# Triangular inverses of the first mixer in three blocks of 42 and 43 rows, with two applications of W, and a new order of the work around them

## The chip, the cores and the metric

The kernel runs on one core of a Trainium2 chip. Its engines work side by side, each on its own queue of instructions: TensorE (PE; its weight loads are shown apart, as PEld), VectorE (DVE), ScalarE (ACT), GpSimd (POOL) and SyncE (SP), which issues most DMAs. The metric is the device time of one execution in microseconds. Every run of the kernel before took between 2796.86 and 2800.05 us.

## The reference

Two layers on 256 tokens of width 2048, in float32. The first layer's mixer is a gated DeltaNet; the change is in that mixer alone. Cut to what matters:

```python
proj = x @ w_in                                  # q, k, v, z, and two gates per value head
qkv = silu(causal_dwconv(qkv, conv_w))           # 16 q/k heads, 32 value heads, 128 wide
q = l2norm(q) * 128 ** -0.5; k = l2norm(k)
gc = cumsum(g)                                   # log-decay within a chunk
lmat = where(strict, (beta * k) @ k.T * exp(gc_i - gc_j), 0)
sol = solve_triangular(I + lmat, [beta * v, beta * k * exp(gc)], lower, unit_diagonal)
# then a scan over chunks with state S, an RMS norm of o, times silu(z), times w_o
```

The two layers go on with LayerNorm, a convolutional GLU, a gated embedding, a second mixer with sparse attention, and again a GLU and the embedding.

## The kernel before

**Weights and matmuls.** A weight chunk of 512 KB is loaded by SP into one of four `raw` tiles, split by ACT into a rounded part `hi` and by DVE into the remainder `lo` (L114, L115; three buffers each), and used by PE. `gemm_t_steps` (L147 with `hi`, L151 with `lo`; tile `mm_ps`) makes transposed products, `gemm_steps` (L184, L187, L190; tile `b_ps`) plain ones. A scheduler sets the order on every engine when the program is built, by its own costs; on the chip each queue runs strictly in that order.

**The mixer.** 32 value heads are worked in eight groups of four (`g` = 0 to 7). The 256 tokens are two halves (`a` = 0, 1) of 128, so that each group has eight triangular matrices `L` of 128x128 (two halves, four heads). For a group: `keys` (gemms for k and q), `zgate` (the z gemm), `values` (the v gemm), and between them the attention arithmetic:

- `decays` and `sums` make decay factors and the norms from the Gram matrix of k (`gram`, L542 and L543); `blocks` finishes `L` on DVE (L574) and sends the four diagonal blocks of 32x32 of each matrix to DRAM (`lt`, four DMAs) and back (`ld`, four DMAs) so that 128 partitions hold 32 blocks in four copies. All eight DMAs stand in SP's queue, among the weight loads.
- `substitute` inverts the blocks on POOL: 31 columns, for each a product `xt` (L612) and a subtraction (L614), starting from an identity `xi` that POOL copies from constants (L609). Four DMAs write the result to `tt`.
- `inverses` brings it back as block-diagonal matrices `pm` (four DMAs on POOL's queue, L631), multiplies `L` by them on PE (`w_ps`, L623) and keeps what lies above the diagonal blocks as `W` (ACT, L638).
- `solve` then needs, for each half, y0 = `pm` x rhs, and three times y = y0 - W y (a product on PE, L623, tile `s_ps`, and a subtraction on DVE, L691): with four blocks in a row, W to the fourth power is zero. The second half waits for the first (`n21`).
- `causal` and `mixes` make the masked q-k products; `outputs` makes o and its norm; its transposes run later as `rest`.

In the loop the work of group n = s+1 that leads to its substitution (`front(n)`) is written after `inverses(s)`, that is, behind the z gemm of group n. A float32 matmul of the attention part (128x128, not rounded) shows as two records in the trace.

Of the kernel before, what the change touches and what calls it, by code (L numbers as in the profile page):

```python
# [30 lines left out]
C_IDENT, C_TRI, C_QMIN, C_CMIN, C_CAUSAL, C_XINIT, C_ONES = 0, 128, 256, 384, 512, 640, 896  # L31
N_CONST = 1024


def constants():

    c = np.zeros((P, N_CONST), np.float32)
    i, j = np.arange(P)[:, None], np.arange(P)[None, :]
    c[:, C_IDENT:C_IDENT + P] = i == j
    c[:, C_TRI:C_TRI + P] = i <= j  # L40
    c[:, C_CMIN:C_CMIN + P] = np.where(j <= i, np.float32(3.4e38), np.float32(-BIG))
    x = np.zeros((4, 32, 8, 32), np.float32)
    for cg in range(4):
        for k in range(8):
            x[cg, :, k, 4 * k + cg] = 1.0
    c[:, C_XINIT:C_XINIT + 256] = x.reshape(P, 256)
    c[:, C_ONES:C_ONES + P] = 1.0
# [16 lines left out]
class Trunk:  # L64
    def __init__(self, nc, tc, ctx, t):

        self.low_last = False
        self.nc, self.tc, self.t = nc, tc, t
        pool = lambda **k: ctx.enter_context(tc.tile_pool(**k))

        self.const = pool(name="const", bufs=1)
        self.hl = pool(name="hl", bufs=3)
        self.xtp = pool(name="xtp", bufs=1)
        self.big = pool(name="big", bufs=1)
        self.cp = pool(name="cp", bufs=1, side="right")
# [289 lines left out]
    def gdn_gates(self, pool, w, gk):  # L365
# [42 lines left out]
        nc.tensor.matmul(pc[:, 64:96], self.ones, g[:, 0], start=True, stop=True)  # L408
# [8 lines left out]
    def gdn(self, ahead):  # L417
# [3 lines left out]
        with tc.tile_pool(name="gk", bufs=1) as gk, tc.tile_pool(name="gw", bufs=1) as pool:  # L421
# [5 lines left out]
            cr = pool.tile([64, 4, P], F32, tag="ld", name="cr")  # L427
            w = pool.tile([P, 1024], F32, tag="L", name="gates")
            def load(nb, to=None):

                for a in range(2):
                    nc.sync.dma_start(out=xs[nb][:, a], in_=t["x"][a * P:(a + 1) * P, nb * 512:(nb + 1) * 512])
                for a in range(2):
                    self.halves = self.to_xT(self.xT, xs[nb][:, a], a, nb * 4, to)
                later = {0: [(w[:, 256 + 32 * i:288 + 32 * i], bass.AP(tensor=t[k].tensor, offset=t[k].offset,
                                                                       ap=[[0, P], [1, 32]]))
                             for i, k in enumerate(("gdn_dt_bias", "gdn_a_log"))],
                         1: [(cr, t["gdn_conv_w"].rearrange("k (n c) -> n k c", c=P)), (self.cst, t["cst"][:, P:]),
                             (ng, t["gdn_norm_g"].rearrange("(p o) -> p o", o=1))]}.get(nb, ())
                for out, src in later:  # L440
                    self.after(nc.gpsimd.dma_start(out=out, in_=src), self.turned, sync=True)
# [11 lines left out]
    def gdn_groups(self, pool, gk, cw, ng, oT, load, taps, gates, ahead):  # L453
# [7 lines left out]
        nc.gpsimd.memset(pm, 0.0)  # L461
        W = pool.tile([P, 2, 4, P], F32, tag="W", name="W")
# [22 lines left out]
        def decays(s):  # L485
# [5 lines left out]
            L = s["L"] = pool.tile([P, 2, 4, P], F32, tag="L", name="L")  # L491
# [4 lines left out]

        def causal(s):

            g, dm = s["g"], s["qd"]
            do = s["qo"] = pool.tile([P, 4, P], F32, tag="qo", name="qo", bufs=2)  # L500
            for h in h4:
                nc.scalar.activation(do[:, h], dm[:, 1, h], AF.Exp, bias=self.gout[:, 4 * g + h:4 * g + h + 1])
            n21 = s["n21"] = pool.tile([P, 4, P], F32, tag="n21", name="n21", bufs=2)
            nc.vector.tensor_tensor(five(n21), bcast(s["gram"][0][:, :, P:S], 2, 2), five(do), op=ALU.mult)
# [5 lines left out]
            sq = s["sq"] = pool.tile([P, 2, S], F32, tag="y0", name="sq")  # L510
            nc.scalar.activation(sq, s["q"], AF.Square)
# [34 lines left out]
        def sums(s):  # L546
# [3 lines left out]
            ss, ik = small("ss", 4), small("ik", 4)  # L550
# [17 lines left out]
        def blocks(s):  # L568
# [8 lines left out]
            lt = self.dr.tile([8, 4, 32, 32], F32, tag="lt", name="lt")  # L577
            for b in range(4):
                nc.sync.dma_start(out=lt[:, b].rearrange("q i j -> i q j"),
                                    in_=L[32 * b:32 * b + 32, :, :, 32 * b:32 * b + 32].rearrange("p a h j -> p (a h) j"))  # L580
            ld = s["ld"] = pool.tile([P, 32, 32], F32, tag="ld", name="ld")
            for e in h4:
                nc.sync.dma_start(out=ld[32 * e:32 * e + 32], in_=bass.AP(tensor=lt.tensor, offset=lt.offset,
                                                                          ap=[[1024, 32], [1, 1024]]))

        def mixes(s):
# [6 lines left out]

            pss = self.sp.tile([P, 4], F32, tag="sp", name="ss_ps")
            for h in range(2):
                for a in range(2):
                    nc.tensor.matmul(pss[:, 2 * h + a:][:, 0:1], s["sq"][:, h, a * P:(a + 1) * P],
                                     self.ones[:, 0:1], start=True, stop=True)
# [4 lines left out]
        def substitute(s):  # L603


            ld = s["ld"]
            xi = pool.tile([P, 8, 32], F32, tag="xi", name="xi", bufs=2)
            tmp = pool.tile([P, 8, 32], F32, tag="xt", name="xt", bufs=2)
            nc.gpsimd.tensor_copy(xi, self.xinit.rearrange("p (c j) -> p c j", c=8))  # L609
            for i in range(31):  # L610
                w, m = 31 - i, i // 4 + 1
                nc.gpsimd.tensor_tensor(tmp[:, :m, :w], bcast(ld[:, i + 1:, i], m, 1),  # L612
                                        xi[:, :m, i:i + 1].to_broadcast([P, m, w]), op=ALU.mult)
                nc.gpsimd.tensor_tensor(xi[:, :m, i + 1:], xi[:, :m, i + 1:], tmp[:, :m, :w], op=ALU.subtract)  # L614
            tt = s["tt"] = self.dr.tile([8, 4, 8, 4, 32], F32, tag="tt", name="tt")
            for e in range(4):
                nc.gpsimd.dma_start(out=tt[:, :, :, e].rearrange("q b c j -> (q b) c j"), in_=xi[32 * e:32 * e + 32])
# [10 lines left out]
        def inverses(s):  # L628

            for b in range(4):  # L630
                nc.gpsimd.dma_start(out=pm[32 * b:32 * b + 32, :, 32 * b:32 * b + 32],  # L631
                                    in_=s["tt"][:, b].rearrange("q c e j -> (c e) q j"))
            for a in range(2):
                ps = self.sp.tile([P, 4, 96], F32, tag="bk", name="w_ps")
                mul(s["L"][:, a], pm[:, 4 * a:4 * a + 4, 32:], ps)

                for b in (1, 2, 3):
                    nc.scalar.activation(W[:32 * b, a, :, 32 * b:32 * b + 32], ps[:32 * b, :, 32 * b - 32:32 * b], AF.Copy)  # L638

        def values(s):  # L640
            g = s["g"]
            v = pool.tile([P, 4, S], F32, tag="v", name="v")
            steps = self.gemm_t_steps(w_in, 4096 + 512 * g, 512, self.xT, conv(32 + 4 * g, lambda n: v[:, n]))
            if not g:
# [18 lines left out]
        def zgate(s, rest):  # L663
# [7 lines left out]
            for j, _ in enumerate(self.gemm_steps(w_in, 8192 + 512 * s["g"], 512, lambda k: self.xT[:, k], KT, done)):  # L671
                if j > 2 and rest:
                    rest.pop(0)()

        def solve(s):
            vt = s["vt"]
            u = s["u"] = pool.tile([P, 2, 4, P], F32, tag="u", name="u")
            for a in range(2):
# [55 lines left out]
        def front(s):  # L734
# [455 lines left out]
```

## Time and profile before

| | us |
|---|---|
| median of three runs (2796.86, 2797.15, 2800.05) | 2797.15 |
| the profiled execution's own time | 2797.12 |
| its span from first to last instruction | 2795.1 |
| PE busy / PEld busy | 2776.6 / 2390.1 |
| DVE busy / ACT busy / POOL busy | 1856.2 / 1421.6 / 337.7 |
| POOL busy in 143 to 228 us (one group's length) | 32.57 |

A busy PE is not PE at its peak: the ends of matmuls are modelled, and neighbours overlap. What one matmul costs is read from the distance of the starts in the timeline. The trace has the device's granted TensorE clock at 1.00 all along.

### The profile page before, as it was taken

To read this page: it belongs to the slowest core of one execution; us is meant where nothing else is said; L and a number is where in the kernel's file an instruction comes from. 1 tells how busy PE (TensorE), PEld (TensorE's weight loads), DVE (VectorE), ACT (ScalarE), POOL (GpSimd) and SP (SyncE) were. 2 spreads that over 40 slices of the span, in tenths; PEclk is the share of its full clock that TensorE was granted. 3 is DMA by queue.
4 is the path that set the end of the run, shared out by engine and by line. 5 is a ranking of instruction groups with operands and counts; after the bars stand their busy time and mean duration, and the time that the engine had idled before them with its cause. 6 is when DMAs were issued, how large, how long until landed. Compare 5 with 4: busy or idle time off the path is not lost. (4 is left out here: it accounts for less than half of the span.)

```text
span 2795.1 us, 40216 instructions
## 1 busy us (share of the span) xinstructions
PE 2776.6 (99%) x14958; PEld 2390.1 (86%) x14958; DVE 1856.2 (66%) x3059; ACT 1421.6 (51%) x2239; POOL 337.7 (12%) x688
## 2 busy tenths in 40 slices
PE   8999999999999999999999999999999999999999
PEld 7888888888888888888888889888888888888887
DVE  6787787877556666666545665776676666655566
ACT  4555566555445555555434544455465555543453
POOL 1543234442200000000000000120000000000000
PEclk9999999999999999999999999999999999999999
DMA  7755665655565666666556567655556666665655
GB/s 213 205 157 158 166 176 164 168 152 159 173 210 164 193 206 206 207 196 207 196 191 208 171 198 215 181 152 163 181 181 196 197 187 199 194 195 195 207 171 195
DMA packets 412275, 520.82 MB, mean 186 GB/s; under 512 B 28940, under 2 KB 301712, under 8 KB 411824
## 3 DMA queue, kind: packets, MB, share of 16 engines
q1 hardware_dynamic: 404912, 499.91, 58.9%
q0 software_dynamic: 7168, 18.35, 2.7%
q8 instruction: 117, 1.92, 0.3%
q14 instruction: 78, 0.64, 0.1%
HBM read 513.94 MB, written 7.39 MB: 187 GB/s over the span
## 5 line engine op out<-in xcount | busy, mean ns | idle before, releaser
L115 DVE TENSOR_TENSOR lo<-raw,hi 128x1024 fp32r<-128x1024 f32 (+1 forms) x921 | 1125.0, 1223 | 606.0 <-ACT hi L114 594.6
L114 ACT ACTIVATE hi<-raw 128x1024 fp32r<-128x1024 f32 (+1 forms) x921 | 967.9, 1053 | 698.9 <-PE b_ps L187 469.5
L147 PE MATMUL mm_ps<-xT,hi 128*128 128x512 f32 (+1 forms) x4176 | 1027.9, 394 | 2.6 <-ACT hi L114 2.3
L147 PEld LDWEIGHTS mm_ps<-xT,hi 128*128 128x128 f32 (+1 forms) x4176 | 762.0, 188 | 148.9 <-ACT hi L114 2.9
L151 PEld LDWEIGHTS mm_ps<-xT,lo 128*128 128x128 f32 (+1 forms) x4176 | 539.4, 191 | 22.7 <-DVE lo L115 1.5
L151 PE MATMUL mm_ps<-xT,lo 128*128 128x256 f32 (+1 forms) x4176 | 557.2, 284 | 0.4 <-DVE lo L115 0.4
L184 PE MATMUL b_ps<-hi,xT 128*128 128x512 f32 (+1 forms) x704 | 270.9, 386 | 0.0
L187 PE MATMUL b_ps<-hi,xT 128*128 128x512 f32 (+1 forms) x704 | 268.8, 383 | 0.0
L220 ACT ACTIVATE fold<-mm_ps 128x256 f32<-128x256 f32 x261 | 98.1, 376 | 268.1 <-PE mm_ps L147 267.8
L184 PE MATMUL b_ps<-hi,hTA 128*128 128x512 f32 x512 | 199.3, 389 | 0.0
L187 PE MATMUL b_ps<-hi,hTA 128*128 128x512 f32 x512 | 199.2, 389 | 0.0
L190 PE MATMUL b_ps<-lo,xT 128*128 128x512 f32 (+1 forms) x704 | 188.4, 383 | 0.0
L239 POOL DMA_DIRECT2D lng<-in_ln_g x16 | 8.8, 547 | 1239.1 <-PE b_ps L190 654.5
L612 POOL TENSOR_TENSOR xt<-ld,xi 128x60 f32<-128x60 f32 (+24 forms) x248 | 116.2, 468 | 345.1 <-DMA ld<-lt 326.3
L187 PEld LDWEIGHTS b_ps<-hi,xT 128*128 128x128 f32 x704 | 132.2, 188 | 24.8
L184 PEld LDWEIGHTS b_ps<-hi,xT 128*128 128x128 f32 x704 | 132.2, 188 | 24.1
L190 PEld LDWEIGHTS b_ps<-lo,xT 128*128 128x128 f32 x704 | 129.9, 188 | 24.5
L190 PE MATMUL b_ps<-lo,hTA 128*128 128x512 f32 x512 | 136.8, 389 | 0.0
L190 PEld LDWEIGHTS b_ps<-lo,hTA 128*128 128x128 f32 x512 | 96.1, 188 | 20.0
L184 PEld LDWEIGHTS b_ps<-hi,hTA 128*128 128x128 f32 x512 | 96.1, 188 | 20.0
L187 PEld LDWEIGHTS b_ps<-hi,hTA 128*128 128x128 f32 x512 | 96.1, 188 | 19.9
L614 POOL TENSOR_TENSOR xi<-xi,xt 128x60 f32<-128x60 f32 (+24 forms) x248 | 107.5, 433 | 19.4
(266 smaller groups left out, 2571.0 us busy)
## 6 DMA issues: line engine op xcount, KB each, us to landing
raw<-in_gdn_w_in SPq DMA_DIRECT2D x193, 512.0 KB, 4.4
raw<-in_ffn_w_gate SPq DMA_DIRECT2D x160, 512.0 KB, 4.4
raw<-in_ffn_w_up SPq DMA_DIRECT2D x160, 512.0 KB, 4.6
raw<-in_ffn_w_down SPq DMA_DIRECT2D x160, 512.0 KB, 4.1
raw<-in_dsa_w_in SPq DMA_DIRECT2D x72, 512.0 KB, 3.7
raw<-in_gdn_w_o SPq DMA_DIRECT2D x64, 512.0 KB, 4.0
raw<-in_ple_w_gate SPq DMA_DIRECT2D x64, 512.0 KB, 4.9
raw<-in_dsa_w_o SPq DMA_DIRECT2D x32, 512.0 KB, 3.9
```

Source lines behind the costliest of these rows:

```text
L114: act = nc.scalar.activation(hi, raw, AF.Copy)
L115: ins = nc.vector.tensor_tensor(lo, raw, hi.bitcast(F32), op=ALU.subtract)
L147: ins = nc.tensor.matmul(q[:m, :], hi[:, k, o:o + m], x[:, k0 + k].rearrange("p a b -> p (a b)"), start=k0 + k == 0, stop=last)
L151: ins = nc.tensor.matmul(q[:m, S:], lo[:, k, o:o + m], x[:, k0 + k, 0, :], start=False, stop=last)
L184: ins = nc.tensor.matmul(ps[a][:, :n], xh, hi, start=k == 0, stop=False)
L187: self.before = nc.tensor.matmul(ps[a][:, :n], xl, hi, start=False, stop=False)
L190: self.last = nc.tensor.matmul(ps[a][:, :n], x(k)[:, 0, a * P:(a + 1) * P], lo, start=False, stop=k == kt - 1)
L220: nc.scalar.activation(t[:m], ps[:, S:], AF.Copy)
L239: ins = self.nc.gpsimd.dma_start(out=r, in_=bass.AP(tensor=src.tensor, offset=src.offset, ap=[[0, P], [1, n]]))
L612: nc.gpsimd.tensor_tensor(tmp[:, :m, :w], bcast(ld[:, i + 1:, i], m, 1), xi[:, :m, i:i + 1].to_broadcast([P, m, w]), op=ALU.mult)
L614: nc.gpsimd.tensor_tensor(xi[:, :m, i + 1:], xi[:, :m, i + 1:], tmp[:, :m, :w], op=ALU.subtract)
```

## The change

Blocks of 32 rows become blocks of 42, 43 and 43 rows (`B_FROM` = 0, 42, 85, 128). Three blocks in a row need two applications of W. The pieces:

- `substitute` runs 42 columns, 84 operations of POOL in place of 62, on up to 132 elements for each partition (76 before). Four copies of 24 blocks lie in groups of 32 partitions, of which eight carry zeros. A block's columns lie in two tiles, 22 and 21 wide, so that `lt` takes six DMAs (48 or 32 rows, pieces of 88 and 84 bytes: 1920 pieces in place of 1024 of 128 bytes), and `ld` eight in place of four.
- `xi` starts from a DMA of constants in place of a copy by POOL. `pm` comes back in three DMAs of 48 rows in place of four of 32; ACT makes two pieces of W in place of three.
- `solve` loses one of three applications in each half.
- `front(n)` now stands at the start of z's gemm of group n (`zgate(n, [], ...)`), and `L` has two buffers. For the first group's successor it stands behind that gemm, and seven of the eight steps of its v gemm are taken before `inverses(0)`.
- `causal`, `squares` and `mixes` of a group move from `front` and from behind `front` into `values`; `cross` (with its own exponentials, four more of ACT for each group) makes `n21` ahead of them. `qo`, `ld` and `ik` have one buffer, `cr` and the ones for one product sit in other tiles.

```diff
+B_ROWS, B_COLS, B_LEFT = 43, 12, 22
+B_FROM = (0, 42, 85, P)
...
-            lt = self.dr.tile([8, 4, 32, 32], F32, tag="lt", name="lt")
-            for b in range(4):
-                nc.sync.dma_start(out=lt[:, b].rearrange("q i j -> i q j"),
-                                    in_=L[32 * b:32 * b + 32, :, :, 32 * b:32 * b + 32].rearrange("p a h j -> p (a h) j"))
...
+            for lt, ld, k, n, o, tall, lead in lds:
+                for b, r in enumerate(B_FROM[:3]):
+                    c = r + o
+                    r0 = min(c, P - tall)
+                    at = lead - c + r0
+                    nc.sync.dma_start(out=lt[8 * b:8 * b + 8, at:at + tall].rearrange("q i j -> i q j"),
+                                      in_=L[r0:r0 + tall, :, :, c:c + n].rearrange("p a h j -> p (a h) j"))
+            for lt, ld, k, n, o, tall, lead in lds:
+                for e in h4:
+                    nc.sync.dma_start(out=ld[32 * e:32 * e + 32], in_=lt[:, lead:lead + k])
...
-            nc.gpsimd.tensor_copy(xi, self.xinit.rearrange("p (c j) -> p c j", c=8))
-            for i in range(31):
-                w, m = 31 - i, i // 4 + 1
...
+            xi = pool.tile([P, B_COLS, B_ROWS], F32, tag="xi", name="xi")
+            nc.gpsimd.dma_start(out=xi, in_=t["cst"][:, C_XINIT:])
+            for i in range(B_ROWS - 1):
+                w, m = B_ROWS - 1 - i, i // 4 + 1
+                col = ld[:, i + 1:, i] if i < B_LEFT else right[:, i + 1 - B_LEFT:, i - B_LEFT]
+                tmp = pool.tile([P, 132], F32, tag="xt", name="xt")[:, :m * w].rearrange("p (c j) -> p c j", c=m)
+                nc.gpsimd.tensor_tensor(tmp, bcast(col, m, 1), xi[:, :m, i:i + 1].to_broadcast([P, m, w]), op=ALU.mult)
+                nc.gpsimd.tensor_tensor(xi[:, :m, i + 1:], xi[:, :m, i + 1:], tmp, op=ALU.subtract)
...
-                for i in range(3):
+                for i in range(2):
                     ps = mul(W[:, a], y)
...
             if g < 7:
                 n = keys(g + 1, rest)
-                zgate(n, [])
+                zgate(n, [], (lambda: front(n)) if g else None)
+                if not g:
+                    front(n)
+                    for _, _ in zip(range(7), begin(n)[0]):
+                        pass
...
             inverses(s)
             if g < 7:
-                front(n)
-                mixes(n)
                 substitute(n)
             solve(s)
```

Where the scheduler now puts the instructions, at three places.

PE, second half of `solve` in the second group, from the product with `n21` to the first product of the outputs. Before (`s_ps<-y` are the applications of W, `s_ps<-vt,pm` makes y0, `mm_ps` is the v gemm of the next group between them):

```order
L623 MATMUL s_ps<-u,n_1522 128x128 x4
L147 MATMUL mm_ps<-xT,hi 128x512 x8
L623 MATMUL s_ps<-vt,pm 128x128 x4
L147 MATMUL mm_ps<-xT,hi 128x512 x2
L151 MATMUL mm_ps<-xT,lo 128x256 x2
L623 MATMUL s_ps<-y_2597,W 128x128 x4
L151 MATMUL mm_ps<-xT,lo 128x256 x8
L623 MATMUL s_ps<-y,W 128x128 x4
L151 MATMUL mm_ps<-xT,lo 128x256 x6
L147 MATMUL mm_ps<-xT,hi 128x512
L623 MATMUL s_ps<-y,W 128x128 x4
L704 MATMUL o_ps<-u,qd 128x128 x4
```

The same stretch now:

```order
L640 MATMUL s_ps<-u,n_1582 128x128 x4
L149 MATMUL mm_ps<-xT,lo 128x256 x4
L145 MATMUL mm_ps<-xT,hi 128x512 x5
L640 MATMUL s_ps<-vt,pm 128x128 x4
L145 MATMUL mm_ps<-xT,hi 128x512 x4
L640 MATMUL s_ps<-y_2761,W 128x128 x4
L145 MATMUL mm_ps<-xT,hi 128x512 x7
L149 MATMUL mm_ps<-xT,lo 128x256 x3
L640 MATMUL s_ps<-y,W 128x128 x4
L743 MATMUL o_ps<-u,qd 128x128 x4
```

One application of four matmuls is gone; between each product and the next there is still work of the v gemm.

PE, at the end of the second z gemm (`b_ps`), where the first group's inverses are first used (`w_ps`). Before:

```order
L190 MATMUL b_ps<-lo,xT 128x512 x2
L623 MATMUL w_ps<-pm,L 128x96 x8
L542 MATMUL g_ps<-k 128x256
L543 MATMUL g_ps<-k 128x128
L542 MATMUL g_ps<-k 128x256
L543 MATMUL g_ps<-k 128x128
L623 MATMUL s_ps<-vt,pm 128x128 x4
```

Now (the Gram matrix of the second group first, then 112 matmuls of its v gemm):

```order
L555 MATMUL g_ps<-k 128x256
L556 MATMUL g_ps<-k 128x128
L555 MATMUL g_ps<-k 128x256
L556 MATMUL g_ps<-k 128x128
L145 MATMUL mm_ps<-xT,hi 128x512 x8
L149 MATMUL mm_ps<-xT,lo 128x256 x16
L145 MATMUL mm_ps<-xT,hi 128x512 x16
L149 MATMUL mm_ps<-xT,lo 128x256 x16
L145 MATMUL mm_ps<-xT,hi 128x512 x16
L149 MATMUL mm_ps<-xT,lo 128x256 x16
L145 MATMUL mm_ps<-xT,hi 128x512 x16
L149 MATMUL mm_ps<-xT,lo 128x256 x8
```

Directly behind these rows follow `w_ps<-pm,L` and `s_ps<-vt,pm`: the first use of `pm` moved behind one Gram product and 56 + 56 matmuls of the v gemm. In later groups `w_ps` stands directly behind the z gemm, as before.

POOL, at the end of a substitution (`tt` goes out, `pm` comes back, the next `xi`). Before:

```order
L612 TENSOR_TENSOR xt<-ld,xi 128x8
L614 TENSOR_TENSOR xi<-xi,xt 128x8
L617 DMA tt<-xi 256x1x32 x4
L631 DMA pm<-tt 32x8x32 x4
L609 COPY xi<-cst 128x256
L612 TENSOR_TENSOR xt<-ld,xi 128x31
```

Now:

```order
L630 TENSOR_TENSOR xt<-ld,xi 128x11
L631 TENSOR_TENSOR xi<-xi,xt 128x11
L634 DMA tt<-xi 384x1x43 x4
L650 DMA pm<-tt 48x8x42
L650 DMA pm<-tt 48x8x43 x2
L625 DMA xi<-in_cst 128x516
L630 TENSOR_TENSOR xt<-ld,xi 128x42
```

One substitution follows the other on POOL as before, with a load of `xi` between them.

More of the change, by code (lines that the diff above doesn't have):

```diff
@@ L41, in constants @@
     c[:, C_CMIN:C_CMIN + P] = np.where(j <= i, np.float32(3.4e38), np.float32(-BIG))
[L42 to L47, printed above, removed]
+    x = np.zeros((4, 32, B_COLS, B_ROWS), np.float32)
+    for n in range(B_ROWS):
+        x[n % 4, :, n // 4, n] = 1.0
+    c[:, C_XINIT:] = x.reshape(P, B_COLS * B_ROWS)
     c[:, C_CAUSAL:C_CAUSAL + P] = j <= i
@@ L407, in gdn_gates @@
         nc.tensor.matmul(pc[:, 0:64], self.tri, g64, start=True, stop=True)
-        nc.tensor.matmul(pc[:, 64:96], self.ones, g[:, 0], start=True, stop=True)
+        ones = pool.tile([P, P], F32, tag="y0", name="ones")
+        nc.gpsimd.memset(ones, 1.0)
+        nc.tensor.matmul(pc[:, 64:96], ones, g[:, 0], start=True, stop=True)
         nc.tensor.matmul(pc[:64, 128:256], g64, self.tri, start=True, stop=True)
@@ L461, in gdn_groups @@
         nc.gpsimd.memset(pm, 0.0)
+        lds, nl = [], B_ROWS - B_LEFT
+        for k, n, o, tall in ((B_ROWS, B_LEFT, 0, 48), (nl, nl, B_LEFT, 32)):
+            lead = B_FROM[2] + o + tall - P
+            lt = self.dr.tile([32, lead + tall, n], F32, tag=f"lt{n}", name="lt", bufs=1)
+            ld = pool.tile([P, k, n], F32, tag=f"ld{n}", name="ld")
+            nc.gpsimd.memset(ld, 0.0)
+            nc.gpsimd.dma_start(out=lt[24:, lead:lead + k], in_=ld[:8])
+            lds.append((lt, ld, k, n, o, tall, lead))
         W = pool.tile([P, 2, 4, P], F32, tag="W", name="W")
@@ L628, in inverses, with begin @@
         def inverses(s):
-            for b in range(4):
-                nc.gpsimd.dma_start(out=pm[32 * b:32 * b + 32, :, 32 * b:32 * b + 32],
-                                    in_=s["tt"][:, b].rearrange("q c e j -> (c e) q j"))
-            for a in range(2):
[L634 to L638, printed above, removed]
+            tt, rows = s["tt"], 4 * B_COLS
+            for b, r in enumerate(B_FROM[:3]):
+                r0, w = min(r, P - rows), B_FROM[b + 1] - r
+                nc.gpsimd.dma_start(out=pm[r0:r0 + rows, :, r:r + w],
+                                    in_=bass.AP(tensor=tt.tensor, offset=tt.offset + (8 * b * rows - r + r0) * B_ROWS,
+                                                ap=[[B_ROWS, rows], [rows * B_ROWS, 8], [1, w]]))
+            r1, r2 = B_FROM[1:3]
+            for a in range(2):
+                ps = self.sp.tile([P, 4, P - r1], F32, tag="bk", name="w_ps")
+                mul(s["L"][:, a], pm[:, 4 * a:4 * a + 4, r1:], ps)
+                for r, n in ((r1, r2 - r1), (r2, P - r2)):
+                    nc.scalar.activation(W[:r, a, :, r:r + n], ps[:r, :, r - r1:r - r1 + n], AF.Copy)
+        def begin(s):
+            g = s["g"]
+            v = pool.tile([P, 4, S], F32, tag="v", name="v")
+            if "v" in s:
+                return s["v"]
+            s["v"] = self.gemm_t_steps(w_in, 4096 + 512 * g, 512, self.xT, conv(32 + 4 * g, lambda n: v[:, n])), v
+            return s["v"]
         def values(s):
             g = s["g"]
-            v = pool.tile([P, 4, S], F32, tag="v", name="v")
-            steps = self.gemm_t_steps(w_in, 4096 + 512 * g, 512, self.xT, conv(32 + 4 * g, lambda n: v[:, n]))
+            steps, v = begin(s)
             if not g:
@@ L649, in values @@
                 front(s)
+                causal(s)
                 substitute(s)
+            else:
+                causal(s)
+                if g > 1:
+                    for _ in range(3):
+                        next(steps)
+                squares(s)
+                next(steps)
+                mixes(s)
             self.go_(steps)
@@ L661, in values, with zgate @@
             return [lambda: turn(0), lambda: turn(1)]
-        def zgate(s, rest):
+        def zgate(s, rest, behind=None):
             zs = s["zs"] = pool.tile([P, 2, 512], F32, tag="zs", name="zs", bufs=2)
@@ L671, in zgate @@
             for j, _ in enumerate(self.gemm_steps(w_in, 8192 + 512 * s["g"], 512, lambda k: self.xT[:, k], KT, done)):
-                if j > 2 and rest:
+                if behind is not None and not j:
+                    behind()
+                if j > 3 and rest:
                     rest.pop(0)()
@@ L738, in front @@
                 blocks(s)
-            causal(s)
+            cross(s)
         n, rest = keys(0), []
@@ L745, in gdn_groups @@
             if not g:
-                rest.insert(0, lambda: mixes(s))
+                rest[:0] = [lambda: squares(s), lambda: mixes(s)]
                 zgate(s, rest)
```

51 lines of the change are left out of this document (22 added, 29 removed).

## The prediction

> **What bounds the kernel now.** I read the page's head first, then who PE waited for, the window of one group, and last the timeline of PE and POOL around one `solve`.
>
> ```profile
> span 2795.1 us, 40216 instructions
> PE 2776.6 (99%) x14958; PEld 2390.1 (86%) x14958; DVE 1856.2 (66%) x3059; ACT 1421.6 (51%) x2239; POOL 337.7 (12%) x688
> ```
>
> ```profile
> PE t_ps L231 <- DMA x_in<-in_x: 5.1, 1, 5.1
> ...
> PE g_ps L542 <- DVE L L574: 0.5, 1, 0.5
> ```
>
> ```profile
> 314.00:399.00 85.00, 84.95 (x504) 74.55 (x503) 66.52 (x146) 48.33 (x102) 32.38 (x71) 1.00 0.60 164
> ```
>
> The waits are for PE: who, total us, times, longest. The window gives PE, PEld, DVE, ACT and POOL busy: a group lasts some 85 us, DVE works 67 of them, ACT 49, POOL 33, and PE has no gap. PE's own issue sets the time, so a PE record that goes is a gain, and work on another engine costs only where PE comes to wait for it.
>
> A busy PE is modelled, so the price of a record is the distance of starts:
>
> ```profile
> 317.23 3.82 PE L147 MATMUL mm_ps<-xT,hi 128*128 128x512 f32 x16
> 320.89 2.08 PE L151 MATMUL mm_ps<-xT,lo 128*128 128x256 f32 x16
> 322.80 1.09 PE L147 MATMUL mm_ps<-xT,hi 128*128 128x512 f32 x4
> ...
> 330.72 1.14 PE L623 MATMUL s_ps<-y,W 128*128 128x128 f32 x8
> 331.62 1.20 PE L151 MATMUL mm_ps<-xT,lo 128*128 128x256 f32 x8
> 332.65 0.63 PE L147 MATMUL mm_ps<-xT,hi 128*128 128x512 f32 x2
> 333.12 1.05 PE L623 MATMUL s_ps<-y,W 128*128 128x128 f32 x8
> 333.93 1.17 PE L147 MATMUL mm_ps<-xT,hi 128*128 128x512 f32 x4
> 334.95 1.16 PE L623 MATMUL s_ps<-u,n 128*128 128x128 f32 x8
> ```
>
> Sixteen `hi` matmuls take 3.66 us (0.229 each), sixteen `lo` 1.91 (0.119 each). An application of W, eight records, takes 331.62 - 330.72 = 0.90, and the eight `lo` behind it take 1.03 in place of 0.95: 0.98 in all where it had to wait a moment for DVE. The one at 333.12 takes 0.81, the four `hi` behind it 1.02 in place of 0.92: 0.91.
>
> **The change part by part.**
>
> *Applications of W.* One of three goes in two halves of eight groups: 16 x (0.91 to 0.98) = 14.6 to 15.7 us of PE; I take 15.1. In the new order every product is still followed by gemm work before its reader, 0.7 us or more (six `lo` are 0.72, four `hi` 0.92), about what stood there before, so the shorter chain makes no new gap. A block of float32 work inserted elsewhere costs only its own records: the change of kind is in the figures above, and there are as many `g`, `ss` and transposing matmuls as before. `w_ps` has as many records, narrower ones.
>
> *The first q-k product.* In group 0 it came late:
>
> ```profile
> 78.30 1.07 PE L190 MATMUL b_ps<-lo,xT 128*128 128x512 f32 x4
> 79.91 0.70 PE L542 MATMUL g_ps<-q,k 128*128 128x256 f32 x2 [0.54 <-DVE L L574]
> ```
>
> Four matmuls at 0.227 end at 79.21, so PE lost 0.7. It now stands twelve and more z matmuls later (2.7 us): -0.7, at worst 0.
>
> *The substitution on POOL.* This is the part that grows.
>
> ```profile
> 337.19 0.26 POOL L612 TENSOR_TENSOR xt<-ld,xi 128x29 f32<-128x29 f32 x1
> 337.52 0.30 POOL L614 TENSOR_TENSOR xi<-xi,xt 128x29 f32<-128x29 f32 x1
> 337.90 1.21 POOL L612 TENSOR_TENSOR xt<-ld,xi 128x28 f32<-128x28 f32 x1
> ...
> 344.22 0.33 POOL L612 TENSOR_TENSOR xt<-ld,xi 128x66 f32<-128x66 f32 x1
> ...
> 346.58 0.35 POOL L612 TENSOR_TENSOR xt<-ld,xi 128x76 f32<-128x76 f32 x1
> ```
>
> ```profile
> 337.78 1.22 DVE L115 TENSOR_TENSOR lo<-raw,hi 128x1024 fp32r<-128x1024 f32 x1
> ```
>
> From 29 to 76 elements an operation goes from 0.26 to 0.35: some 2.3 ns an element on 0.18 us, with 0.08 between operations. The one at 337.90 took 1.21: it began inside DVE's split of 337.78 and ended 0.11 after it. The Trainium skill, "SBUF — State Buffer", section "SBUF: two separate sides", has this as an exclusive lock of a port pair that GpSimd shares with DVE operations with two SBUF inputs; the row agrees for POOL. By that rule a longer substitution collides with more splits; without it, it would be 38 us long, and the wait worked out below would be nought.
>
> Before, 62 operations on 2 x 1560 elements make 11.2 + 7.2 + 5.0 = 23 us, and the second group's took this long:
>
> ```profile
> 164.98 0.26 POOL L612 TENSOR_TENSOR xt<-ld,xi 128x31 f32<-128x31 f32 x1 [29.72 <-DMA ld<-lt]
> ...
> 196.84 0.32 POOL L614 TENSOR_TENSOR xi<-xi,xt 128x8 f32<-128x8 f32 x1
> 197.46 2.32 POOL L617 DMA_DIRECT2D tt<-xi  x4 [0.29 <-POOL xi L614]
> 202.42 2.33 POOL L631 DMA_DIRECT2D pm<-tt  x4 [2.64 <-PE mm_ps L147]
> ```
>
> That is 32.2 us, of which 9 lost to collisions, 0.15 an operation. Now 84 operations on 2 x 3663 elements: 15.1 + 16.8 + 6.7 = 38.6. With the loss per operation 51, with the loss as a share of the time (28%) 54: I take 52. As 52 of the 84 are larger than any in the trace, and read columns of another stride, I keep 48 to 58.
>
> From the end of a substitution to `pm` landed: 197.16 to the last issue's start at 204.17, and the landing:
>
> ```profile
> DMA to landing us min/median/max: 3.2/4.7/6.6
> ```
>
> 11.7 in all; one `pm` issue fewer (0.6) against larger pieces: kept.
>
> *Is it in time?* POOL's deadline is `w_ps` on PE:
>
> ```profile
> 138.80 1.92 PE L623 MATMUL w_ps<-pm,L 128*128 128x96 f32 x16
> 140.55 0.62 PE L542 MATMUL g_ps<-k 128*128 128x256 f32 x2
> ```
>
> ```profile
> 224.16 1.92 PE L623 MATMUL w_ps<-pm,L 128*128 128x96 f32 x16
> ```
>
> Group 0:
>
> ```profile
> 89.23 0.78 POOL L612 TENSOR_TENSOR xt<-ld,xi 128x31 f32<-128x31 f32 x1 [25.91 <-DMA ld<-lt]
> ...
> 125.28 0.22 POOL L614 TENSOR_TENSOR xi<-xi,xt 128x8 f32<-128x8 f32 x1
> ```
>
> Its deadline goes to 138.8 - 0.7 + 1.3 (Gram, four pieces) + 56 x 0.229 + 56 x 0.119 = 158.9. Its `ld` is unchanged but for two more `lt` issues, so 89.7 + 55 (this group had 36.3 us, 4 more than the next) + 11.7 = 156.4. In time by 2.5 us.
>
> Group 1: the Gram product comes at 138.1, and `ld` landed 24.4 us behind it before (140.55 to 164.98). DVE is freer there now (`causal` went), SP has more to issue; kept: 162.5. POOL is free by then: 144.7, `tt` and `pm` out at 153, `xi` in some 4 us later. 162.5 + 52 + 11.7 = 226.2. The deadline: 224.16 - 0.7 - 1.9 (two applications) + 1.3 (group 2's Gram product now stands ahead) = 222.9. PE waits 3.3 us; with 48 to 58 us nought to 9.3.
>
> Later groups: `front` runs at the start of z's gemm, some 20 us sooner before its deadline, against 20 us more of substitution. From Gram product to deadline are a period of 83.5 (85.4 from one `w_ps` above to the next, less 1.9) and 20 of the z gemm, the chain is 24.4 + 52 + 11.7 = 88: 15 us to spare. A rewritten `ld` must also wait until the last substitution has read it; SP, with weights queued behind, asks for it some 80 us after the last one, when POOL has been done for 10 or more.
>
> *SP's queue.* Six `lt`, one `raw`, eight `ld` now stand in the z stage. The second group's before, and how long `lt` and `ld` took to land (min, median, max):
>
> ```profile
> 153.17 2.06 SPq L579 DMA_DIRECT2D lt<-L  x4
> 158.29 0.39 SPq L109 DMA_DIRECT2D raw<-in_gdn_w_in  x1
> 159.01 1.71 SPq L583 DMA_DIRECT2D ld<-lt  x4
> 161.52 0.39 SPq L109 DMA_DIRECT2D raw<-in_gdn_w_in  x1
> ```
>
> ```profile
> DMA to landing us min/median/max: 4.2/4.5/5.2
> ```
>
> SP was bound for 8.3 us with one weight load in between; now some 11. A z chunk is 12 x 0.227 = 2.7 us of PE, so loads come up to 5 us late. ACT waited for PE's release of `hi` there, not for DMAs:
>
> ```profile
> ACT hi L114 <- PE b_ps L187: 66.6, 50, 4.8
> ```
>
> Four `raw` tiles are 10.9 us ahead, three `hi` and `lo` on top: 0, at worst 1 us.
>
> *The rest at nothing.* DVE loses 16 subtractions of 0.69; ACT gains 32 exponentials and loses 16 copies of W; both have 18 us or more free of 85, and PE waits for neither but in `solve`. The new memsets and loads on POOL at the start lie in PE's 5.1 us of waiting for x. Behind the mixer the order is the same.
>
> Sum: -15.1 - 0.7 + 3.3 = -12.5 on the profiled execution's 2797.12 (the median is 2797.15): 2784.6 us.
>
> **The rivals.**
> - *No wait at all.* The substitution takes 48 us or `ld` comes 3 us sooner. -15.8: 2781.3.
> - *A longer wait.* The Trainium skill, "DMA: Bandwidth & Descriptors", section "Why small descriptors are slow (HBM only)", puts a fixed cost on each packet; no row here prices pieces of 88 bytes. As a mechanism here: `lt`'s landing, 5.2 us behind its first issue for 1024 pieces, would be 9.7 for 1920, the wait 7.8, and the time 2789.1. Speaks against it: the landing before is mostly the same for four DMAs issued over 2 us. A substitution of 56 to 58 us gives the same.
> - *No change.* Waits eat 10 to 21 us: by the substitution at 59 to 65 us, or by 1.5 us in each group because weights come late behind SP's longer queue. 2795.
> - *Slower: POOL becomes the bound of the first two groups.* A second substitution starts no sooner than 11.2 us after the first has ended (5.3 to the first `pm` issue, 1.8 for three, some 4 for `xi`), so with s for its length `pm` of group 1 is there at 100.9 + 2s + 11.7, a wait of 2s - 110.3 once s is over 62. At s = 63 the gain is gone, at 66 the kernel is 0.2% slower; at 70, 2811. For it: the largest operations are not in the trace. Against: 0.26, 0.33, 0.35 lie on a line.
>
> **How the numbers follow.** Runs agree so well that 0.2%, 5.6 us, is about what can be told from no change. A wait of 1 to 7 us: 50%, 2782 to 2788.5, forecast 2784.6. No wait: 25%. A longer wait, still faster by over 0.2% (below 2791.5): 8%. Within 0.2%: 10%. Slower: 7%. Faster is thus 0.83. The range 2780 to 2791.5 holds the first three.
>
> **What would show it.** PE records of `s_ps<-y,W` go from 384 to 256, and `hi`, `lo` and `b_ps` keep their prices. A group lasts some 83.5 us. A substitution lasts 52, of group 0 55. PE waits at `w_ps` of the second group by about 3 us and at no other; the row before it shows the gap. Wrong would be: waits at `w_ps` in every group, PE waiting for `hi` in the z gemms, or a substitution over 60 us.

## The result and the profile after

The changed kernel takes 2819.0 us (median of four runs, 2817.28 to 2819.45) against 2797.2 before: ratio 1.0075, 95% interval 1.0057 to 1.0092. It is 22 us slower, where 12.5 us less was forecast. The profiled execution took 2818.87 us.

The head of the profile after:

```profile
span 2817.1 us, 40248 instructions
PE 2770.4 (98%) x14830; PEld 2384.9 (85%) x14830; DVE 1876.8 (67%) x3043; ACT 1427.6 (51%) x2255; POOL 479.9 (17%) x861
```

PE has 128 records fewer, as foreseen, and is busy 6 us less in a span that is 22 us longer: it stands still 28 us more. For what, the waits of PE say (who, total us, times, longest):

```profile
PE w_ps L640 <- DMA pm<-tt: 14.5, 2, 11.0
PE g_ps L556 <- ACT vt L696: 14.0, 6, 2.9
PE t_ps L229 <- DMA x_in<-in_x: 5.0, 1, 5.0
PE b_ps L182 <- DVE pd L219: 2.0, 2, 1.6
```

The first two lines are new, and the fourth was 0.8 us before. All of the loss lies in the first mixer: the first `p_ps` behind it starts at 801.14 us before and at 822.45 now (+21.3 of the +22.0 in the span).

**The wait at `w_ps`.** PE and POOL in the timeline at the first group's inverses:

```profile
156.27 1.11 PE L149 MATMUL mm_ps<-xT,lo 128*128 128x256 f32 x8
168.43 3.69 PE L640 MATMUL w_ps<-pm,L 128*128 128x86 f32 x16 [11.04 <-DMA pm<-tt]
171.91 1.98 PE L640 MATMUL s_ps<-vt,pm 128*128 128x128 f32 x8
```

```profile
147.72 1.19 POOL L631 TENSOR_TENSOR xi<-xi,xt 128x11 f32<-128x11 f32 x1
149.21 2.50 POOL L634 DMA_DIRECT2D tt<-xi  x4 [0.29 <-POOL xi L631]
163.33 1.91 POOL L650 DMA_DIRECT2D pm<-tt  x3 [11.62 <-DMA tt<-xi]
165.23 0.58 POOL L625 DMA_DIRECT2D xi<-in_cst  x1
170.98 0.28 POOL L630 TENSOR_TENSOR xt<-ld,xi 128x42 f32<-128x42 f32 x1 [5.17 <-DMA xi<-in_cst]
```

PE was there at 157.3, POOL finished at 148.9, and `pm` landed at 168.3: the 19 us between are transfers. The second of the two waits is the last group's:

```profile
747.34 3.69 PE L640 MATMUL w_ps<-pm,L 128*128 128x86 f32 x16 [3.46 <-DMA pm<-tt]
```

**The wait in z's gemm.** In each of groups 2 to 7 PE stops one matmul behind the first tile of the Gram product:

```profile
301.52 0.58 PE L182 MATMUL b_ps<-hi,xT 128*128 128x512 f32 x1
304.98 0.71 PE L556 MATMUL g_ps<-k 128*128 128x128 f32 x4 [2.88 <-ACT vt L696]
305.45 0.59 PE L185 MATMUL b_ps<-hi,xT 128*128 128x512 f32 x1
305.84 0.63 PE L182 MATMUL b_ps<-hi,xT 128*128 128x512 f32 x1
```

ACT in the same stretch:

```profile
302.45 0.88 ACT L696 ACTIVATE vt<-v_ps,sv 128x128 f32<-128x128 f32 x3
303.20 1.07 ACT L112 ACTIVATE hi<-raw 128x1024 fp32r<-128x1024 f32 x1
304.15 0.52 ACT L485 ACTIVATE ac<-pd,cw 128x256 f32<-128x256 f32 x1
304.55 0.38 ACT L696 ACTIVATE vt<-v_ps,sv 128x128 f32<-128x128 f32 x1
```

The second Gram tile takes over a PSUM buffer (tag `sp`, two buffers) from the transposed v, and ACT copies the last quarter of that out only at 304.55, behind a split and a piece of a convolution. By distances of starts the gaps are 1.9, 3.2 and four times 2.7 us, 16.1 in all.

**What follows a gap.** The 16 `w_ps` records after the first gap take 3.48 us to the next row, where 1.75 was usual. Windows ahead of, in and behind that gap (the number ahead of the last two is the granted TensorE clock):

```profile
157.00:168.00 11.00, 0.38 (x4) 0.18 (x2) 1.96 (x3) 1.01 (x1) 2.48 (x4) 0.74 1.04 154
168.00:176.00 8.00, 7.57 (x36) 7.60 (x36) 0.00 (x0) 1.61 (x5) 3.99 (x14) 0.50 0.61 201
176.00:190.00 14.00, 13.95 (x101) 12.29 (x100) 10.99 (x20) 6.51 (x18) 12.18 (x24) 1.00 0.23 64
```

For 7.6 us after it PE runs at half its clock. Distances of starts over the usual distance of their kind give 3.9 us lost there, 3.1 behind the last group's gap, and 1.7 behind each of two of the six Gram gaps; behind the other four the rate was full. Together: gaps of 11.2 + 16.1 + 3.6 = 30.9 and 10.4 at half clock, 41.3 us, and 1.3 more in two waits for `pd` in the output gemm. Against that stand 14.0 for the applications, 1.5 between 50 and 100 us (the q-k product's gap of 0.7, 0.3 in the rows behind it, and a gap of 0.5 at 58.6, all gone), 0.8 in the first 28 us (a gap of 0.6 at 23.7 that is gone, and x 0.2 sooner), and some 5 in small moments, which I did not follow: 21.3.

Which of the Gram gaps led to half clock does not follow from their length. The granted clock changes at 162.3, 176.0, 305.7, 309.1, 565.1, 568.5, 746.0 and 752.8, all whole multiples of 3.41 us apart. Here are two such steps around the gap at 301.5, which was followed by half clock, and two around the one at 389.4, which was not:

```profile
302.30:305.70 3.40, 0.72 (x5) 0.72 (x6) 3.08 (x6) 2.63 (x7) 1.04 (x2) 0.99 0.94 206
305.70:309.10 3.40, 3.40 (x9) 2.61 (x9) 2.68 (x13) 0.83 (x2) 0.00 (x0) 0.50 0.93 229
387.60:391.00 3.40, 2.35 (x11) 1.66 (x9) 3.40 (x7) 3.00 (x8) 0.37 (x1) 1.00 0.96 229
391.00:394.40 3.40, 2.07 (x11) 1.81 (x12) 3.09 (x8) 1.70 (x4) 0.00 (x0) 1.00 0.98 142
```

The first gap lies inside one step, in which PE is busy 0.72 us; the second is cut in two by a boundary. With all 13 traces cut into such steps, and PE's standing still counted by the modelled ends of its matmuls, each of the 27 steps at full clock in which PE stood still for 1.9 us or more was followed by one at 0.50, and of the 20 with 1.3 to 1.8 us one was (1.6 us, in the run on `tt`). This is a pattern in the traces; no run moved a gap against the steps on purpose.

The chain from one group's Gram product to its inverses, by the starts and landings in the traces:

| us | Gram | first `lt` issued | `ld` landed | substitution | `pm` landed | `w_ps` | to spare |
|---|---|---|---|---|---|---|---|
| before, group 3 | 311.2 | 323.9 | 335.7 | 335.8 to 367.9 | 380.4 | 394.9 | 14.5 |
| before, group 7 | 652.7 | 665.3 | 677.4 | 677.6 to 709.7 | 721.8 | 726.5 | 4.8 |
| after, group 0 | 58.4 | 78.8 | 94.1 | 91.7 to 148.9 | 168.3 | 168.4 | waits |
| after, group 1 | 136.4 | 149.6 | 168.1 | 171.0 to 220.2 | 235.6 | 238.1 | 2.6 |
| after, group 3 | 300.9 | 320.0 | 334.2 | 333.3 to 385.2 | 402.4 | 411.8 | 9.3 |
| after, group 7 | 647.6 | 664.8 | 679.0 | 677.9 to 730.6 | 747.2 | 747.3 | waits |

The first step of the chain, from the Gram product to the first `lt`, is DVE's. The eight operations that finish `L` in group 3, before and after:

```profile
L574 DVE SCALAR_TENSOR_TENSOR L<-g_ps,c,L x8: 341/342/348, 318.9 to 323.3; 128x128 f32<-128x128 f32 x8
```

```profile
L587 DVE SCALAR_TENSOR_TENSOR L<-g_ps,c,L x8: 337/340/345, 315.5 to 319.6; 128x128 f32<-128x128 f32 x8
```

They start 7.6 us behind the Gram product before and 14.6 behind it now.

The chain's transfers, by the table of DMA issues (KB each, median us from issue to landing), before and after:

```profile
lt<-L SPq DMA_DIRECT2D x32, 32.0 KB, 4.3
tt<-xi POOLq DMA_DIRECT2D x32, 32.0 KB, 2.6
```

```profile
tt<-xi POOLq DMA_DIRECT2D x32, 64.5 KB, 7.4
lt<-L SPq DMA_DIRECT2D x24, 33.0 KB, 7.4
lt<-L SPq DMA_DIRECT2D x24, 21.0 KB, 7.0
```

### The profile page after: what moved, and what is told of

Same layout as the page of the kernel before. It is cut to its first block, busy times and chain, and to the rows that moved or that the text cites. A ratio compares the mean times of both kernels' runs of the same rounds, so it can differ in the third digit from the quotient of the medians.

```text
span 2817.1 us, 40248 instructions
## 1 busy us (share of the span) xinstructions
PE 2770.4 (98%) x14830; PEld 2384.9 (85%) x14830; DVE 1876.8 (67%) x3043; ACT 1427.6 (51%) x2255; POOL 479.9 (17%) x861
## 5 line engine op out<-in xcount | busy, mean ns | idle before, releaser
L630 POOL TENSOR_TENSOR xt<-ld,xi 128x120 f32<-128x120 f32 (+5 forms) x336 | 183.4, 546 | 182.3 <-DMA ld<-lt 151.4
L631 POOL TENSOR_TENSOR xi<-xi,xt 128x120 f32<-128x120 f32 (+5 forms) x336 | 183.3, 546 | 26.4
```

What stands on the lines that cost most here:

```text
L630: nc.gpsimd.tensor_tensor(tmp, bcast(col, m, 1), xi[:, :m, i:i + 1].to_broadcast([P, m, w]), op=ALU.mult)
```

## The experiments

All start from the changed kernel (2819.0); the kernel before measured 2796.8 to 2797.2 beside each set (medians; single executions 2795.4 to 2798.8).

**The Gram product's buffer, alone.** DVE, ACT, POOL and SP keep their order word for word.

```diff
-        def gram(k, y):
+        def gram(k, y, tag="sp"):
...
-            p2 = self.sp.tile([P, 2, P], F32, tag="sp", name="g2_ps")
+            p2 = self.sp.tile([P, 2, P], F32, tag=tag, name="g2_ps")
...
-            s["gram"] = gram(s["k"], s["k"])
+            s["gram"] = gram(s["k"], s["k"], "bk" if s["g"] > 1 else "sp")
```

> Theory (a PSUM buffer): in groups 2 to 7 the second Gram tile waits in z's gemm for the buffer that ACT empties late (vt), six gaps of 1.9 to 3.2 us, 16.1 us in all, and after two of them the granted clock halves for 1.7 us of loss each. With that tile in another pair of buffers and nothing else moved on DVE, ACT, POOL or SP, the six gaps are gone: 2819.0 - 16.1 - 3.4 = 2799.5 us, kept 2797 to 2804 since w_ps of the last group may wait longer. Rival (the z gemm is held by ACT's late work in any case, or the Gram product by k): the gaps stay or come back at the next reader of the same buffers (mixes, hi), and the time stays over 2812.

Measured: 2803.1 (2796.2 to 2804.5; ratio to before 1.0018, 1.0009 to 1.0028). The line of `g_ps` is gone from PE's waits, and a group now lasts 83.0 us with PE busy throughout (forecast: 83.5). One period, from `w_ps` to `w_ps`:

```profile
319.30:402.30 83.00, 83.00 (x489) 73.08 (x488) 69.36 (x146) 49.16 (x104) 50.58 (x92) 1.00 0.68 178
```

15.9 us came from one PSUM tag. `lt` still starts 17.3 to 17.5 us behind the Gram product in groups 3 to 7 (12.7 before), so that this part of the chain is not the gap's. The last group's gap grew from 3.6 to 6.6, since its work came up sooner by the gaps and its chain did not by as much.

**The substitution of the first two groups, shortened.** The kernel leaves out 22 of the 42 columns there, so that these inverses are incomplete.

```diff
-            for i in range(B_ROWS - 1):
+            for i in range(B_ROWS - 1 if s["g"] > 1 else 20):
```

> Leaves out 22 of the 42 columns of the substitution in the first two groups (wrong inverses there). Theory (POOL too late for the first w_ps): substitution 0 falls from some 57 to 25 us, the gap of 11.2 us ahead of w_ps in group 0 is gone with the 3.9 us at half clock behind it, and nothing takes its place in group 1: 2819.0 - 15.1 = 2803.9 us, kept 2801 to 2807. Rival 1 (the clock loss does not come from the gap): 2807.8. Rival 2 (the gap is a transfer's, not POOL's): the gap stays above 5 us, 2810 or more. The gaps of the Gram product stay at 16 us in all three.

Measured: 2802.3 (2799.0 to 2805.8): 16.7 us less, where the theory gave 15.1. No gap at `w_ps` of groups 0 and 1; the Gram gaps stay, 14.1 in all by distances of starts. PE's waits:

```profile
PE g_ps L556 <- ACT vt L696: 11.9, 6, 2.4
PE w_ps L640 <- DMA pm<-tt: 3.8, 1, 3.8
```

The last of these is the last group's. The run shortens both groups; group 0 alone would hardly have done it. In the changed kernel `pm` of group 1 lands at 235.6, and `w_ps` of group 1 comes at 238.1 only because PE lost 11.2 + 3.9 us at group 0. Without that loss it would come at about 223.0 and wait some 12.6 us, an estimate from these numbers.

**Both**, again without the 22 columns.

> The edits of the two runs ahead together (22 columns left out in the first two groups). Theory: the two causes add, 2819.0 - 19.5 - 15.1 = 2784.4 us, which is what the prediction gave with hardly a wait left; 2782 to 2789. What stays is the wait of 3.6 us at w_ps of the last group with 3 us at half clock. Rival (a third cost of the change, hidden so far under the two gaps): 2790 or more.

Measured: 2788.7 (2787.2 to 2790.7; ratio 0.9969, 0.9958 to 0.9981). The gains are 15.9, 16.7 and together 30.3. What is left is the last group, whose gap is 5.4 us here with 2.9 behind it:

```profile
PE w_ps L640 <- DMA pm<-tt: 5.2, 1, 5.2
```

Without those 8.3 us it would be 2780.4; the prediction's case with no wait was 2781.3. So the arithmetic of PE's own work stood to about 1 us, and the difference lies in the three waits (first `w_ps`, Gram products, last `w_ps`) with their clock. The 2780.4 is a subtraction; this kernel was not run.

**The gaps filled, not removed**, with products of `ident` with itself (`idle`).

```diff
+            if s["g"] in (0, 7):
+                idle(12 if s["g"] else 40, self.last if s["g"] else self.tail)
...
+                if k is y and not j and n["g"] > 1:
+                    idle(8, self.last)
```

> Fills the gaps and takes none away: 40 idle float32 products (9.0 us) ahead of the first w_ps, 8 (1.8 us) ahead of each Gram product of groups 2 to 7, 12 (2.7 us) ahead of the last w_ps, on operands that nobody reads. Theory (the clock halves because PE stood still): the waits for data end when they did, but the rows behind them keep their full rate: 3.9 + 1.7 + 1.7 + 3.1 = 10.4 us less, 2808.6, kept 2806 to 2812. Rival (the doubled distances behind the gaps are transfers or PSUM traffic): within 2 us of 2819, or more, where an idle product delays something.

Measured: 2810.4 (2809.9 to 2812.8), 8.6 less. The same three windows:

```profile
157.00:168.00 11.00, 11.00 (x99) 10.96 (x97) 2.79 (x3) 1.34 (x2) 2.47 (x4) 1.00 0.87 156
168.00:176.00 8.00, 8.00 (x59) 7.02 (x58) 2.02 (x4) 2.34 (x7) 6.01 (x19) 1.00 0.64 198
176.00:190.00 14.00, 13.71 (x97) 12.35 (x97) 12.39 (x27) 8.70 (x30) 12.20 (x24) 1.00 0.40 114
```

With useless work in the gap PE has 59 records in the 8 us behind it, where it had 36, at a clock of 1.00, while the weights move beside it as before (DMA share 0.64 against 0.61). The half clock comes from PE's standing still. The Trainium skill names the same effect, "TensorE: Matmul & The Clock Gate", section "HAM oscillation — how this bites in real kernels": no gaps over some 3.4 us. The traces agree on the halving, but not on the length: gaps of 2.5 and 2.8 us led to it in the shortened run, others of 2.7 did not. The steps of 3.41 us shown above tell these apart too (2.2 and 2.3 us of standing still in one step against at most 1.8).

**Three applications again.**

```diff
-                for i in range(2):
+                for i in range(3):
...
-                    y = u[:, a] if i else pool.tile([P, 4, P], F32, tag="y", name="y", bufs=2)
+                    y = u[:, a] if i == 2 else pool.tile([P, 4, P], F32, tag="y", name="y", bufs=2)
```

> Three applications of W in place of two (the third gives the same sum), all else as in the changed kernel. If an application is worth on PE what the prediction took, 16 x 0.91 to 0.98 us = 15.1 come back, less up to 1.9 at the wait for the last group's inverses, which stand behind one more solve: 2819 + 13 to 15 = 2832 to 2834. Rival (an application lies under other work in the new order, or leaves PE waiting for DVE): under 2826 or over 2838.

Measured: 2820.4 (2819.8 to 2821.7): only 1.4 more, the rival. Yet the records themselves came back at full price; of after, and of this run:

```profile
L640 PE MATMUL s_ps<-y,W 128*128 128x128 f32 x256 | 36.6, 287 | 0.1
```

```profile
L640 PE MATMUL s_ps<-y,W 128*128 128x128 f32 x384 | 54.6, 285 | 0.3 <-DVE y L730 0.3
```

By distances of starts they take 14.0 us more. The Gram gaps fell from 16.1 to 6.8 us with no half clock behind them, and the last group's gap is gone: PE did the extra work in time in which it had waited. A gap of 2.0 ahead of `ot_ps` at 209.3 and 3.4 us at half clock from 718.5 are new. Here, taking PE work away had bought longer waits. The same edit where PE waits little beside the first `w_ps`, on the version of the next paragraph:

> The version with more cover, with three applications of W in place of two. That version has no waits at the Gram products and slack at every w_ps but the first, so nothing else can absorb the work: theory, an application costs 14 to 15.7 us over the sixteen halves as it did in the records of the run with three (14.0): 2794.5 + 14.5 = 2809, kept 2807 to 2811. Rival (an application is largely hidden in the new order): under 2802.

Measured: 2809.5 (2807.2 to 2810.8) against 2794.5 with two: 14.9 us, inside the forecast and next to the prediction's 15.1.

**More cover, with the Gram product's buffer.** For the first two groups PE is given work ahead of `w_ps`; the last one stands behind four more steps of the output gemm.

```diff
-            for j in range(6):
+            for j in range(8):
...
+                if g < 2:
+                    for i, _ in zip(range(3 if g else 8), begin(n)[0]):
+                        if not g and i == 1:
+                            front(n)
```

> A version that computes all of the reference: second Gram tile of groups 2 to 7 in the other pair of buffers; 16 steps of the output gemm in place of 12 ahead of the last inverses; all eight steps of the second group's v gemm ahead of the first inverses, its Gram product behind the second of them; three steps of the third group's v gemm ahead of the second inverses. Theory: no gap at the Gram products; w_ps of the last group has 10.9 us more in front of it (its wait was 3.6 to 6.6); w_ps of group 0 has 5.5 more, and its tt lands by 155 since lt comes behind it, so pm by 162 against 163; w_ps of group 1 about 238 with pm at 237. With no waits left 2788.7 of the shortened run less 5.4 and 2.9 at half clock = 2780.4, kept 2778 to 2788. Rival (the tail of 19 us behind the first substitution is not the meeting of lt and tt): a gap of 5 us at the first w_ps with 2 to 4 us at half clock, 2788 or more.

Measured: 2794.5 (2792.4 to 2797.0; ratio 0.9992, 0.9983 to 1.0001): the rival, by the gap and the time. The last group's gap is gone, the first is half as long:

```profile
165.94 3.68 PE L640 MATMUL w_ps<-pm,L 128*128 128x86 f32 x16 [5.50 <-DMA pm<-tt]
```

`lt` now starts at 154.5, near the end of `tt`, which lands within 7.8 us (13.4 in the changed kernel): that the two had met was real. But `pm` then meets `lt` and lands 8.5 us after its issue (5.0 there), so the tail is 17.0 and not 13. A new gap of 2.1 us stands ahead of `ot_ps` at 204.8, where the v gemm's steps are missing that had covered DVE, with 3.4 us at half clock behind it.

**The second group's front in its z gemm**, on the version with more cover, and `xi` loaded ahead of `pm` (`unit`).

```diff
-                zgate(n, [], (lambda: front(n)) if g else None)
+                zgate(n, [], (lambda: front(n)) if True else None)
...
             tt, rows = s["tt"], 4 * B_COLS
+            if s["g"] < 7:
+                units.append(unit())
```

> As the run with more cover, but the second group's front (Gram product, L, lt) stands at the start of its z gemm like those of later groups, some 22 us sooner, and xi is loaded ahead of the pm issues. Theory: the second substitution starts right behind the first's tail at about 161, pm of group 1 lands at about 226 against 238, and tt of group 0 meets no lt: 2780, kept 2778 to 2786. Rival (SP's queue): ld of group 1 waits in SP's queue until the first substitution has read the old one, some 8 to 10 us, the weights behind it come late and PE waits for hi: 2784 to 2790, with a gap at hi before 160.

Measured: 2798.3 (2795.8 to 2800.0), outside both ranges. The second substitution starts at 160.7 and `pm` of group 1 lands at 224.5, as the theory said, 22 us early; PE never waits for `hi` there. But PE arrived at the first `w_ps` at 151.6 with 13.7 us to wait, since the scheduler put less of the v gemm ahead of it in this order. The gain went to the wrong group.

**The old place of the front with the new blocks** (one execution).

```diff
             if g < 7:
+                front(n)
                 substitute(n)
```

> The new blocks with the old place of the front: Gram product, L, lt and ld of a group behind the z gemm and the inverses of the group ahead. Theory: the chain from Gram product to pm measured 98 us in the changed kernel, so that w_ps comes no sooner than 100 us after the one ahead, in place of 83: seven waits of 15 to 17 us and 3 to 4 us each at half clock, less the six gaps of the Gram product: 2819 + 130 - 20 = some 2930, kept 2890 to 2960. Rival (the chain is 88 us as the prediction worked it out): waits of 4 to 6 us, 2840 to 2860.

Measured: 2916.9, as the theory had it. PE waits at every group:

```profile
PE w_ps L640 <- DMA pm<-tt: 113.9, 8, 18.9
```

So the longer substitution needs the new place of the front, which was worth some 98 us here; with the old place the new blocks are 120 us slower than the kernel before. The rest of the new order was not tried alone.

**What `tt` costs by the piece** (on the version with more cover). `pm` is read as before, so that the rows of the inverses come back in another order; the transfers have the same bytes.

```diff
-            tt = s["tt"] = self.dr.tile([32, B_COLS, 4, B_ROWS], F32, tag="tt", name="tt")
+            tt = s["tt"] = self.dr.tile([32, 4, B_COLS, B_ROWS], F32, tag="tt", name="tt")
...
-                nc.gpsimd.dma_start(out=tt[:, :, e], in_=xi[32 * e:32 * e + 32])
+                nc.gpsimd.dma_start(out=tt[:, e], in_=xi[32 * e:32 * e + 32])
```

> The version with more cover, with the substitution's result written to tt in runs of 2064 bytes (128 pieces) in place of 172 (1536 pieces); pm is read as before, so its rows come back in another order (a wrong result). Theory (what is written to DRAM is priced by the piece): tt lands some 4 to 5 us after its first issue in place of 8 to 10, the tail from substitution to pm falls from 16 to 11 or 12 in every group, the gap of 5.7 us at the first w_ps falls to about 1 and its 3.3 us at half clock go: 2794.5 - 8 = 2786.5, kept 2784 to 2790. Rival (the landing is set by the weights that are loaded beside it): tt stays at 8 to 10 and the time at 2793 to 2796.

Measured: 2790.1 (2788.7 to 2792.0), at the edge of what was expected. The same bytes in longer runs:

```profile
tt<-xi POOLq DMA_DIRECT2D x32, 64.5 KB, 3.6
```

7.4 us became 3.6, all four of a group land in 4.1 to 6.1 us in place of 7.3 to 13.4. From the first `tt` issue to `pm` the tail of groups 2 to 7 is 11.6 to 12.9, as before the change (10.5 to 12.8; 14.5 to 16.9 in the changed kernel). The first gap is 1.7 with full clock behind it. Part of the rest is a gap of 1.8 us at the second `w_ps` with 3.4 us at half clock behind it: there `pm` took 9.6 us.

**A faster version.** The version with more cover, group 1's Gram product a step later, four steps of the third group's v gemm ahead, and the first outputs' turns in the z gemm:

> The version with more cover, computing all of the reference, with the second group's Gram product one step later (behind the third of its v gemm's eight steps), four in place of three steps of the third group's v gemm ahead of the second inverses, and the turns of the first outputs in z's gemm of the third group in place of its k and q gemms. Theory: lt of group 1 no longer meets pm of group 0, which lands by 163 (gap at the first w_ps 5.7 to 2.5), and the 2.1 us ahead of ot_ps at 204.8 with 1.5 at half clock behind them are gone: 2794.5 - 3.2 - 3.6 - 0 to 3 = 2785 to 2788, kept 2783 to 2791. Rival (group 1's substitution ends later by the step and its w_ps waits): 2790 to 2794 with a gap at the second w_ps.

Measured: 2791.4 (2789.2 to 2794.8; ratio 0.9981, 0.9972 to 0.9990): 5.4 us faster than the kernel before and 27.6 faster than the changed one. That is just outside the forecast (2783 to 2791), and the rival's sign, a gap at the second `w_ps`, did not come. The first gap fell to 3.9, not 2.5: `lt` was issued at 156.4 and `pm` at 157.0, so that the two still met, and `pm` took 8.0 us.

## Why the prediction was wrong, point by point

- *Applications of W, -15.1: right.* 14.0 and 14.6 us by their records, just under the sum's 14.6 to 15.7, and 14.9 by the time, where PE waits little.
- *First q-k product, -0.7: right*; 0.3 us more came from the rows behind that gap, which had been slow at a granted clock of 1.00.
- *Substitution of 52 us, 55 in group 0: right.* 51.8 to 52.7 in groups 2 to 7, 57.2 in group 0, 49.2 in group 1.
- *From its end to `pm`, 11.7, "kept": wrong.* 15 to 17 us, 19 in group 0. I weighed "one `pm` issue fewer (0.6) against larger pieces" and never counted `tt`, whose pieces went from 1024 of 128 bytes to 1536 of 172.
- *`ld` 24.4 us behind the Gram product, kept for group 1 and later: wrong.* It took 31 to 33, for two reasons. First, `lt`: in groups 2 to 7 the six land 8.8 to 11.2 us after the first issue, the four before within 5.1 to 5.6, and in group 1, beside `tt`, 13.5. The rival *a longer wait* had named 9.7 us by the piece. I held against it that the landing was flat over four issues; those four had all their pieces of one size, so this spoke neither way. That the piece sets `lt`'s time is argued; only `tt` was run with longer pieces. Second, in groups 2 to 7 the first `lt` is issued 16 to 19 us behind the Gram product, where 12.7 was usual. DVE finishes `L` that much later at the new place: in group 3 its first operation on the Gram product starts 5.4 us behind that (1.4 before), with pieces of a convolution ahead of it in its queue. The run with the other PSUM buffer shows 17.3 to 17.5 without the gap. "DVE is freer there now" says nothing of the order in DVE's queue. In group 1 this part held (13.2).
- *Group 0 in time by 2.5 us: wrong.* PE was there 1.6 us sooner than worked out (157.3), `pm` 11.9 later: `ld` by 2.0, the substitution by 2.2, the tail behind it by 7.7. Group 1, forecast to wait 3.3, did not wait, but only because group 0's gap had delayed PE: its deadline of 222.9 is met by 238.1 less the 15.1 lost, while its `pm` came at 235.6 and not 226.2 (`ld` 5.6 later, 2.9 until `xi` had landed, the substitution 2.8 shorter, the tail 3.7 longer).
- *Later groups 15 us to spare: wrong in size, 9 to 13 us, and for the last group in kind.* Nothing in my working separated group 7, which has an output gemm's 12 steps in place of the next group's k, q and z. The trace of before shows it with 4.8 us to spare where groups 1 to 6 have 13.5 to 16.
- *"The rest at nothing": wrong, and the largest single miss (16.1 us and 3.4 at half clock).* I moved the Gram product on paper as PE records and as a chain for POOL, and did not ask which PSUM buffer it takes at its new place and who empties that. ACT's free 36 us in 85 are no help when the copy stands behind others in its queue. The price of SP's longer queue, 0 to 1 us, held: PE waits 1.6 us for `hi`, once, at the start of the kernel, and 2.3 before; never in a z gemm.
- *Price of a wait: missing.* Each gap at `w_ps` cost a third again or more, at half clock. The trace of before could not show it: behind its first 12 us its longest gap in the mixer is 1.0 us, at a granted clock of 1.00.

The rival that ended on the slower side named the first two groups, with POOL's length as its trigger (62 us and more) and the wait in group 1. What happened was a wait of that kind in group 0, with a substitution of 52 to 57 and longer transfers, beside a wait that no case had. None of the three signs of being wrong came: the prediction had no sign for a buffer.

## What to carry to other kernels

When a step moves, list for each of its tiles the buffer it takes, the last reader of what lies there, and where that reader stands in its own queue; free engine time says nothing about it. Where small blocks are written to DRAM, count the pieces before and after, and check a deadline for the first and the last turn of a loop apart from the middle. An edit that removes PE work is worth its records only where PE does not wait behind it.

## What the runs showed of the hardware

- A write to DRAM of 172-byte pieces took 7.4 us to land, the same bytes in 2064-byte runs 3.6. The reads back were no slower after than before (`ld` 4.5 before and 2.4 to 3.0 after, `pm` 4.7 and 3.7 to 4.6). The Trainium skill, "DMA: Bandwidth & Descriptors", section "Why small descriptors are slow (HBM only)", gives a fixed cost for each packet. Here it shows on a write; no run changed the pieces of a read alone.
- Two small-piece transfers that meet slow each other: `tt` of group 0 landed within 13.4 us beside `lt`, within 7.8 and 6.2 in two versions where `lt` came later (7.3 to 9.9 in the other groups of the changed kernel).
- The granted clock changed at whole multiples of 3.41 us and stood at 0.50 in the step behind each one in which PE had stood still for 1.9 us or more (27 of 27 in 13 traces). After a gap of 3.2 us PE ran 3.4 us at half clock, after one of 11.2 us 7.6. Of the six gaps of 1.9 to 3.2 us in the changed kernel the two that lay inside one step by 2.3 us or more led to it.
